# Layer two's weights as scaled float16 halves, the attention's split ahead by GpSimd and kept in DRAM

## The chip, the core and the metric

The kernel runs on one core of a Trainium2 chip. A core has five engines with an instruction queue each: TensorE (PE, matrix multiplication; its weight loads are shown apart as PEld), VectorE (DVE), ScalarE (ACT), GpSimd (POOL) and SyncE (SP), which here issues every DMA. Data lies in SBUF (128 partitions), PE writes into PSUM banks, and inputs, outputs and scratch lie in DRAM. The metric is the device time of one execution in microseconds (us). Before the change it is 1198.7 us, the median of three runs (1198.53 to 1199.05).

## What is computed

A trunk of two layers over 1024 tokens of width 1024. Each layer projects its input with `w_in` (1024 x 3072: main, memory queries, main gate, memory gate), runs a main mixer and a cross-attention of four heads into 256 memory tokens, gates both and projects them with `w_out`; then comes a residual and a layer norm.

```python
def mixer_sublayer(x, mem, w_in, w_mem_kv, w_out, main_fn):
    h = x @ w_in
    u_main = h[..., :D_MAIN]
    q_mem = h[..., D_MAIN:D_MIX]
    g_main = h[..., D_MIX:D_MIX + D_MAIN]
    g_mem = h[..., D_MIX + D_MAIN:]
    y_main = main_fn(u_main)
    y_mem = memory_attention(q_mem, mem, w_mem_kv)
    y = jnp.concatenate([y_main * jax.nn.silu(g_main), y_mem * jax.nn.silu(g_mem)], axis=-1)
    return y @ w_out
...
    x = layer_norm(ALPHA * x + y, ln_g[layer], ln_b[layer])
```

Layer one's main mixer is a causal pooling over four windows with a linear map for each group of channels. Layer two's is FoX, attention of 16 heads of 64 with a forget gate: `logit[t,s] = q_t.k_s/8 + cum[t] - cum[s]` for s up to t, where `cum` is the running sum of log-sigmoid gates. Keys, values and gates come from one projection of layer two's input, `w_kv_shared`.

## The kernel before

**Products of float32 accuracy.** A float32 matrix is split into a high and a low part, and a product is three matmuls: high x high, low x high, high x low (`three`, L217). High parts are float32r, low parts bfloat16. A split is an ACT cast for the high part and a DVE subtraction for the low one (`hi_lo`, L186); in FoX both are done by POOL (`gp_hi_lo`, L198), because `low[0]` is true there.

**Slabs.** A slab (L233) is 128 output columns of a projection, for all tokens: its weight (512 KB) is loaded by SP in two pieces of 256 KB, each split as above, and 48 matmuls of 512 columns follow, 24 for each half of the tokens (L253), into the two `pj` banks of PSUM. Layer two has 38 slabs: 24 of `w_in`, 8 for keys and 6 for values; the values of the first two pairs of heads come with the gates from a projection of 272 columns (`v_first`, L830). Layer two's input stands turned (channels in the partitions) in `XH` (float32r) and `XL` (bfloat16), made by `turned_rows` (L342) from each of eight row tiles after the layer norm: two float16 halves, two DMA transposes, and three passes by ACT, DVE and POOL (L351 to L353) into `XH` and `XL`.

**Order of the work.** Layer one's pool groups and its memory attention fill the first 327 us, `out_proj.rest` (L558) with the layer norm reaches to 454, layer two's memory queries and memory projections to 518, memory attention to 588, the first values' projection to 611, the slabs of the first keys and queries to 638; then FoX runs to about 1085, with the remaining slabs between its own matmuls, and layer two's output projection follows. PE's instructions run in the order in which the code issues them (`manual_schedule`); a planner orders the other engines' queues, and each queue runs strictly in order. In memory attention the gates' slabs 20 to 23 are filled in between the steps of the attention; a step is one tile of 128 tokens, with its softmax for four heads (L429 to L440).

**FoX's start.** For each head the running sums are read back into all partitions (tile `R`), POOL masks the diagonal block of `R` (`affine_select`, L978), and DVE adds `R` to the logits and takes the running maximum (L986). The logits lie in three PSUM banks named `L`.

Of the kernel before, what the change touches and what calls it, by code (L numbers as in the profile page):

```python
# [18 lines left out]
P = 128  # L19
S = 1024  # L20
# [22 lines left out]
class InPlace(tuple):  # L43

    pass

# [53 lines left out]
def trunk_kernel(ctx, tc, x, xT, memT, win, wk, wv0, wv, wmk, wmv, wout, poolw, pscale, lng, lnb, bforget, out):  # L100
# [107 lines left out]

    ident = const.tile([P, P], F32, name="ident")
# [23 lines left out]
    def slab(pieces_dram, XH, XL, evac, banks=("pj", 2), make=wt):  # L233

        ready = isinstance(pieces_dram, list)
        if ready:
            ws = pieces_dram
        else:
            ws = [split_w(pieces_dram[0], [P, 4, P], make=make)]
            yield 0  # L240
            ws.append(split_w(pieces_dram[1], [P, 4, P], make=make))
            yield 0

        def terms(n, kts):
            cols = slice(n * NH, (n + 1) * NH)
            out = []
            for kt in kts:
                h, l = ws[kt // 4]
                out.append(three((h[:, kt % 4, :], cut(l, slice(None), kt % 4)), (XH[:, kt, cols], cut(XL, slice(None), kt, cols))))
            return out  # L250

        def put(acc, a, b, start, stop):
            nc.tensor.matmul(acc, a, b, start=start, stop=stop)  # L253
            since[0] += NH

# [11 lines left out]
        for n in range(2):  # L267
# [5 lines left out]
            for j, (a, b) in enumerate(order):  # L273
                put(acc, a, b, j == 0, j == len(order) - 1)
                if j == len(order) - 1:
                    evac(slice(n * NH, (n + 1) * NH), acc)
                yield NH
# [3 lines left out]
    def gate(acc, dst):  # L281

        nc.scalar.activation(dst, acc, AF.Tanh, scale=0.5)
        nc.vector.scalar_tensor_tensor(dst, dst, 1.0, acc, ALU.add, ALU.mult)  # L284

    def mem_kv(l):
# [11 lines left out]
        def project(w_dram):  # L298
# [3 lines left out]
            for pc in range(2):  # L302
                a, b = split_w(w_dram[pc], [P, 4, P], nc.gpsimd if l and not pc else nc.vector)
# [13 lines left out]
        def vals(h):  # L317
            scaled_halves(
                project(wmv[l, h]), [two[:, h, 2 * e : 2 * e + 2, :].rearrange("p m t -> p (m t)") for e in range(2)],
                undo[:, h : h + 1],  # L320
# [6 lines left out]
    def scaled_halves(u, halves, un, by_tile=lambda t: t):  # L327
# [9 lines left out]
        nc.vector.tensor_scalar(un, e, 2.0 ** -15 / PSCALE, None, ALU.mult)  # L337
# [4 lines left out]
    def turned_rows(z, rows, scale, XH, XL, half, whole):  # L342

        sc, un = scale
        hi, lo = (half() for _ in range(2))
        nc.scalar.activation(hi, z, AF.Copy, scale=sc)
        nc.vector.scalar_tensor_tensor(lo, z, sc, hi, ALU.mult, ALU.subtract)
        t = whole()
        nc.sync.dma_start_transpose(t[:, :KT, :], hi)
        nc.sync.dma_start_transpose(t[:, KT:, :], lo)  # L350
        nc.scalar.activation(XH[:, :, rows], t[:, :KT, :], AF.Copy, scale=un)  # L351
        nc.vector.tensor_scalar(XL[0][:, :, rows], t[:, KT:, :], un, None, ALU.mult)
        nc.gpsimd.tensor_scalar(XL[1][:, :, rows], XH[:, :, rows].bitcast(F32), 1.0, 1.0, ALU.mult, ALU.mult)  # L353

    def norm_scale(gb):
# [10 lines left out]
        nc.vector.tensor_scalar(un[:, 1:2], e, 2.0 ** -14, None, ALU.mult)  # L366
        return un[:, 0:1], un[:, 1:2]

    def gate_units(w_dram, dst, XH, XL):
        return slab(w_dram, XH, XL, lambda cols, acc: gate(acc, (dst[0] if isinstance(dst, list) else dst)[:, cols]))  # L370

    def mem_attention(l, XH, XL, kv, qtile, ytile, yd):
# [3 lines left out]
        def query_units(h, make):  # L376
            qh, ql = qs[h]
            return slab(win[l, 8 + h], XH, XL, lambda cols, acc: hi_lo(qh[:, cols], cut(ql, slice(None), cols), acc), make=make)

        def aside_homes():  # L380

            lows = sb([P, 4, 4, P], "P", 5, BF16)
            for n in range(2):
                highs = sb([P, 2, 4, P], "P", 5, F32R)
                left = [[highs[:, k], lows[:, 2 * n + k]] for k in range(2)]
                yield lambda shape, dt=F32R, left=left: left[0].pop(0) if dt == F32R else left.pop(0)[0]

        if l:
            homes = aside_homes()
            units = [query_units(h, wt if h < 2 else next(homes)) for h in range(MH)]  # L390
            for two in units:
                run(islice(two, 2))
            while turns:
                turns.pop(0)(lambda: vt([P, D], F16), lambda: vt([P, 2 * KT, P], F16))
            for two in units:
                run(islice(two, 3 * KT))
            kv = mem_kv(l)
        (kh, kl, v, undo), keys, vals = kv
        for h in range(MH):
# [4 lines left out]
            else:  # L404
                qs.append(in_place(qtile, [P, S]))
                run(query_units(h, wt))
# [7 lines left out]
        for h in range(MH):  # L414
            fill.add(gate_units(win[l, 20 + h], gs[h], XH, XL), SLAB)
# [57 lines left out]
    class OutProj:  # L473
# [63 lines left out]
        def ordered(self, order, c):  # L537
            firsts, lasts = ({id(acc): j for j, (acc, _) in way} for way in (reversed(list(enumerate(order))), enumerate(order)))
            for j, (acc, (y, w)) in enumerate(order):
                nc.tensor.matmul(  # L540
                    acc, y, w, start=c == 2 and j == firsts[id(acc)] and acc is not self.seeded,
                    stop=c == 1 and j == lasts[id(acc)], skip_group_check=acc is self.seeded,
                )
# [14 lines left out]
        def rest(self, resid, XH, XL, dst):  # L558
# [14 lines left out]
            for sp, c in order + [(sp, c) for sp in range(2, ST // 2) for c in (2, 0, 1)]:  # L573
# [12 lines left out]
                for turn in turns if c == (1 if at_end else 0) else ():  # L586
                    turn(lambda: sb([P, D], "raw", 4, F16), lambda: T([P, 2 * KT, P], F16))
                turns = [] if c == 1 else turns
                if at_end and c == 0:
# [6 lines left out]
    def norm(sp, accs, gb, resid, scale, XH, XL, dst, seeded):  # L596
        turns = []
        for a in range(2):
# [30 lines left out]
            if XH is not None:  # L629

                def turn(half, whole, z=z, rows=rows):
                    turned_rows(z, rows, scale, XH, XL, half, whole)
# [47 lines left out]
    with tc.tile_pool(name="in0", bufs=1) as in0:  # L680
# [65 lines left out]
        for g in range(1, 4):  # L746
            pool_group(g)
            out_proj.split((4, 12, 12)[g - 1])

        XH1, XL1 = xs()  # L750
        turns = out_proj.rest(x, XH1, XL1, x1)
# [3 lines left out]
    XH, XL = XH1, XL1  # L755
    with tc.tile_pool(name="in1", bufs=1) as in1:
# [497 lines left out]
```

## Time and profile before

| | us |
|---|---|
| median of three runs | 1198.7 |
| profiled execution | 1198.79 |
| its span in the profile | 1197.0 |
| PE busy | 1172.2 |
| DVE busy | 800.5 |
| ACT busy | 616.9 |
| POOL busy | 208.4 |

The span is what the profile shows of the execution; the rest of its time lies around it. Busy time counts instructions only, not waits. In lists of instructions, the columns are: start and duration in us, engine, line of the code, operation, output and inputs by the program's names, shapes, number of instructions put together, and in brackets the idle time before them with what ended it. In groups the columns are line, engine, operation, names, shapes and number, then busy time in us and the mean of one in ns, then the idle time before them. In tables by stage a pair is busy time and number of instructions, in the order PE, PEld, DVE, ACT, POOL; behind them stand PE's granted clock (1.00 is full), the DMA engines' busy share and GB/s.

### The profile page before, as it was taken

How to read it: one execution, taken by the hardware profiler on the slowest of the kernel's cores; microseconds unless marked ns; L12 is line 12 of the kernel's file. 1: busy time of each engine (PE TensorE's matmuls, PEld its weight loads, DVE VectorE, ACT ScalarE, POOL GpSimd, SP SyncE). 2: the span in 40 equal slices, each digit the busy share in tenths (PEclk: the TensorE clock that was granted, in tenths of full speed). 3: DMA queues.
4: the chain of work that ended last, by engine and by line, in shares of the span. 5: the costliest groups of instructions: out<-in, count | busy, mean ns of one | idle time of the engine just before them, and what ended most of it. 6: DMA issues, size and time to landing. Idle time of an engine off the chain costs nothing. (4 is left out here: it accounts for less than half of the span.)

```text
span 1197.0 us, 19472 instructions
## 1 busy us (share of the span) xinstructions
PE 1172.2 (98%) x6810; PEld 739.3 (62%) x6927; DVE 800.5 (67%) x1864; ACT 616.9 (52%) x1330; POOL 208.4 (17%) x312
## 2 busy tenths in 40 slices
PE   9999999999999999999999999999999999999997
PEld 4567665555555555677776666666666666655554
DVE  6544767374656576377546888778878888874654
ACT  7433654262532224366325777767766787773110
POOL 2000000000000000200103334333334324530000
PEclk9999999999999999999999999999999999999999
DMA  7333654242355666355526789879897999976431
GB/s 246 115 101 87 131 115 159 79 123 80 102 197 158 159 156 161 106 138 100 171 54 161 152 199 173 195 155 195 187 186 164 195 191 210 230 206 229 154 116 48
DMA packets 280803, 182.06 MB, mean 152 GB/s; under 512 B 225024, under 2 KB 238976, under 8 KB 280704
## 3 DMA queue, kind: packets, MB, share of 16 engines
q1 hardware_dynamic: 280704, 180.81, 62.0%
q8 instruction: 54, 0.88, 0.3%
q14 instruction: 45, 0.37, 0.1%
HBM read 95.24 MB, written 22.61 MB: 98 GB/s over the span
## 5 line engine op out<-in xcount | busy, mean ns | idle before, releaser
L253 PE MATMUL pj<-A,w 128*128 128x512 bf16 (+1 forms) x1817 | 571.4, 398 | 2.2 <-DVE B L894 1.1
L253 PE MATMUL pj<-A,wl 128*128 128x512 bf16 x929 | 351.8, 380 | 6.4 <-issue 3.4
L253 PEld LDWEIGHTS pj<-A,w 128*128 128x128 f32 x944 | 174.8, 188 | 45.4 <-POOL wl L200 2.0
L253 PEld LDWEIGHTS <-w 128*128 128x128 bf16 x960 | 93.1, 98 | 121.3 <-issue 39.4
L253 PEld LDWEIGHTS <-wl 128*128 128x128 bf16 x960 | 94.3, 98 | 87.9 <-issue 4.2
L994 ACT ACTIVATE T<-MK,s 128x512 f32<-128x512 f32 x192 | 111.0, 578 | 44.5 <-DVE s L986 22.6
L1015 ACT ACTIVATE P<-T,s 128x512 f16<-128x512 f32 x192 | 103.1, 576 | 52.8 <-issue 26.3
L1016 DVE SCALAR_TENSOR_TENSOR P<-T,s,P 128x512 f16<-128x512 f32 x192 | 112.3, 612 | 24.0 <-ACT P L1015 22.3
L540 PEld LDWEIGHTS <-T 128*128 128x128 bf16 x736 | 70.6, 98 | 88.9 <-issue 6.8
L190 DVE TENSOR_TENSOR wl<-raw,w 128x512 bf16<-128x512 f32 (+1 forms) x96 | 67.9, 713 | 72.3 <-ACT w L189 69.7
L231 PE MATMUL L<-B,B 128*128 128x512 f32 (+3 forms) x384 | 109.0, 386 | 4.6 <-DVE s L986 4.2
L189 ACT CAST w<-raw 128x512 fp32r<-128x512 f32 (+1 forms) x104 | 62.8, 609 | 84.0 <-PE pj L253 57.6
L231 PEld LDWEIGHTS L<-B,B 128*128 128x128 f32 x384 | 71.1, 189 | 29.6 <-DVE s L986 9.9
L353 POOL TENSOR_SCALAR A<-A 128x1024 bf16<-128x1024 f32 x8 | 8.4, 1049 | 444.5 <-ACT A L351 427.9
L986 DVE CUSTOM_DVE_ANT_0 MK<-L,R 128x512 f32<-128x512 f32 (+3 forms) x128 | 72.8, 569 | 8.4 <-PE L L231 5.6
L978 POOL TENSOR_SCALAR_AFFINE_SELECT R<-R 128x128 f32<-128x128 f32 x128 | 42.2, 335 | 207.4 <-DVE s L986 162.5
L200 POOL TENSOR_TENSOR wl<-raw,w 128x512 bf16<-128x512 f32 x54 | 69.4, 1285 | 3.8
L190 DVE TENSOR_TENSOR T<-T,T 128x1024 bf16<-128x1024 f32 x23 | 31.6, 1374 | 48.1 <-ACT T L189 48.0
L189 ACT CAST T<-T 128x1024 fp32r<-128x1024 f32 x23 | 24.1, 1047 | 71.7 <-DMA T<-y1d 45.4
L199 POOL TENSOR_SCALAR w<-raw 128x512 fp32r<-128x512 f32 x54 | 35.9, 665 | 58.5 <-PE pj L253 58.5
L540 PE MATMUL L<-B,T 128*128 128x512 bf16 (+1 forms) x163 | 43.1, 391 | 0.3
L433 ACT ACTIVATE P<-L,s 128x256 f32<-128x256 f32 x64 | 29.6, 474 | 23.4 <-issue 13.0
(296 smaller groups left out, 1789.7 us busy)
## 6 DMA issues: line engine op xcount, KB each, us to landing
raw<-in_win_dram SPq DMA_DIRECT2D x94, 256.0 KB, 2.9
raw<-in_wout_dram SPq DMA_DIRECT2D x40, 256.0 KB, 2.9
B<-B SPq DMA_DIRECT2D x32, 256.0 KB, 4.5
R<-cumd SPq DMA_DIRECT2D x16, 512.0 KB, 4.6
T<-y0d SPq DMA_DIRECT2D x12, 512.0 KB, 5.1
y0d<-Y SPq DMA_DIRECT2D x11, 512.0 KB, 2.7
T<-y1d SPq DMA_DIRECT2D x11, 512.0 KB, 4.7
raw<-in_wmk_dram SPq DMA_DIRECT2D x16, 256.0 KB, 2.7
```

Source lines behind the costliest of these rows:

```text
L189: pin(nc.scalar.copy(hi, src))
L190: pin(by.tensor_tensor(lo[0], src, hi.bitcast(F32), ALU.subtract))
L199: nc.gpsimd.tensor_scalar(hi, src, 1.0, 1.0, ALU.mult, ALU.mult)
L200: nc.gpsimd.tensor_tensor(lo[0], src, hi.bitcast(F32), ALU.subtract)
L231: nc.tensor.matmul(acc, a, b, start=i == 0, stop=i == len(terms) - 1)
L253: nc.tensor.matmul(acc, a, b, start=start, stop=stop)
L540: nc.tensor.matmul(acc, y, w, start=c == 2 and j == firsts[id(acc)] and acc is not self.seeded, stop=c == 1 and j == lasts[id(acc)], skip_ ...
L978: nc.gpsimd.affine_select(R[:, qs], R[:, qs], [[-1, P]], ALU.is_ge, -NEG, base=0, channel_multiplier=1).ins
L986: nc.vector.tensor_tensor_reduce(p[:, lo:up], lg, R[:, lo:up], 1.0, top, ALU.add, ALU.min, m[:, n : n + 1])
L994: nc.scalar.activation(e, p[:, lo:up], AF.Exp, bias=top, scale=-1.0, accum_out=sums[:, n, hd % 2, i : i + 1],)
L1015: nc.scalar.activation(pair[:, lo:up], e, AF.Copy, scale=r)
L1016: nc.vector.scalar_tensor_tensor(pair[:, L + lo : L + up], e, r, pair[:, lo:up], ALU.mult, ALU.subtract)
```

## The change

**Float16 halves in layer two.** `turned_rows` transposes the two float16 halves straight into one tile `X1`, so that the three passes behind the transposes are gone. All of layer two's slabs and `v_first` take float16 halves of the weights too, scaled by one power of two for all weights. The three matmuls stay three, now all float16, with the tokens' side read as four strips of 128. The scale is undone where each product is evacuated.

**The scale.** `look_over` loads all 38 slabs and the four pieces of the first values' projection once more, in layer one, and DVE takes each one's largest magnitude: 16 loads lie beside pool groups one and two, 26 beside the output projection. `weight_scale` brings the maxima of the partitions together through DRAM.

**Split ahead.** `prepared` takes 27 slabs in the order in which FoX needs them. For each, POOL issues the load, multiplies by the scale, rounds to float16, subtracts, and issues the store of both halves to DRAM. FoX then loads halves in place of raw weights, and POOL's splits there are gone. The other 11 slabs are split by ACT and DVE as they are used. Two smaller things move from POOL to DVE: eight subtractions in the memory projections, and the building of the constant tiles `later` and `ones`.

```diff
+    def split_f16(src, make):
+        t = make()
+        hi, lo = t[:, 0], t[:, 1]
+        nc.scalar.activation(hi, src, AF.Copy, scale=wscale[0])
+        nc.vector.scalar_tensor_tensor(lo, src, wscale[0], hi, ALU.mult, ALU.subtract)
+        return hi, (lo, hi)
...
+    def prepared(spare):
+        waiting, lows = [], []
+        def stored():
+            key, out = waiting.pop(0)
+            nc.gpsimd.dma_start(ready[key][0].ap.rearrange("c p e k m -> p c e (k m)"), out)
+        for n, key in enumerate(in_order()):
...
+            with tc.issue_after(lows[n - 3]) if n > 2 else nullcontext():
+                nc.gpsimd.dma_start(r, src.rearrange("c p k m -> p c (k m)"))
+            sc = wscale[0].unsqueeze(2).to_broadcast([P, 2, NH])
+            nc.gpsimd.tensor_tensor(r, r, sc, ALU.mult)
+            nc.gpsimd.tensor_scalar(out[:, :, 0], r, 1.0, 1.0, ALU.mult, ALU.mult)
+            lows.append(nc.gpsimd.tensor_tensor(out[:, :, 1], r, out[:, :, 0], ALU.subtract).ins)
+            waiting.append((key, out))
+            if len(waiting) > 2:
+                with tc.issue_after(lows[-1]):
+                    stored()
+            yield
...
-    def turned_rows(z, rows, scale, XH, XL, half, whole):
-        sc, un = scale
-        hi, lo = (half() for _ in range(2))
-        nc.scalar.activation(hi, z, AF.Copy, scale=sc)
-        nc.vector.scalar_tensor_tensor(lo, z, sc, hi, ALU.mult, ALU.subtract)
-        t = whole()
-        nc.sync.dma_start_transpose(t[:, :KT, :], hi)
-        nc.sync.dma_start_transpose(t[:, KT:, :], lo)
-        nc.scalar.activation(XH[:, :, rows], t[:, :KT, :], AF.Copy, scale=un)
-        nc.vector.tensor_scalar(XL[0][:, :, rows], t[:, KT:, :], un, None, ALU.mult)
-        nc.gpsimd.tensor_scalar(XL[1][:, :, rows], XH[:, :, rows].bitcast(F32), 1.0, 1.0, ALU.mult, ALU.mult)
+    def turned_rows(z, tile_of, sc, X, half):
+        for e in range(2):
+            t = half()
+            if e == 0:
+                hi = t
+                nc.scalar.activation(hi, z, AF.Copy, scale=sc)
+            else:
+                nc.vector.scalar_tensor_tensor(t, z, sc, hi, ALU.mult, ALU.subtract)
+            nc.sync.dma_start_transpose(X.t[:, e, tile_of], t)
...
+    def look_over():
...
+        def reduced():
+            n, t = landed.pop(0)
+            nc.vector.tensor_reduce(tops[:, n : n + 1], t, AX.X, ALU.max, apply_absolute_value=True)
...
-                a, b = split_w(w_dram[pc], [P, 4, P], nc.gpsimd if l and not pc else nc.vector)
+                a, b = split_w(w_dram[pc], [P, 4, P], nc.vector)
...
-        nc.gpsimd.memset(ones, 1.0)
-        nc.gpsimd.memset(later, 0.0)
-        for k in range(1, ST):
-            nc.gpsimd.affine_select(later, later, [[1, P]], ALU.not_equal, 1.0, base=-k * HEADS, channel_multiplier=-1)
+        nc.vector.memset(ones, 1.0)
+        nc.vector.memset(later, 0.0)
+        for k in range(HEADS, P, HEADS):
+            nc.vector.tensor_tensor(later[:, k:], later[:, k:], ident[:, : P - k], ALU.add)
...
             run(start_units(*own, keys))
+            run(prep[0])
+            prep[0] = None
             low[0] = True
             fox(following, out_proj)
```

POOL's queue before, from the end of layer one to FoX's first mask (`L978 AFFINE_SELECT R`). `L353` is the last pass of a turned row, `L190` a subtraction of the memory projections, `L774` to `L777` build the constant tiles, `L199` and `L200` split the first weight pieces for FoX:

```order
L353 TENSOR_SCALAR A_3076<-A_3075 128x8x128 x8
L190 TENSOR_TENSOR wl_4334<-raw_4331,w_4333 128x512
L190 TENSOR_TENSOR wl_4374<-raw_4371,w_4373 128x512
...
L774 MEMSET G_5564 128x128
L775 MEMSET G_5564 128x128
L777 AFFINE_SELECT G_5564<-G_5564 128x128 x7
L199 TENSOR_SCALAR w_6164<-raw_6162 128x512
L200 TENSOR_TENSOR wl_6165<-raw_6162,w_6164 128x512
L199 TENSOR_SCALAR w_6170<-raw_6168 128x512
L200 TENSOR_TENSOR wl_6171<-raw_6168,w_6170 128x512
L978 AFFINE_SELECT R_6139<-R_6139 128x128
```

The same stretch of POOL's queue after the change; the mask is now at L1157. `L271` is a load's issue, `L273` the multiplication by the scale (`unrow`), `L274` the rounding, `L275` the subtraction, `L263` a store's issue; the rows left out are the items between the first and the last:

```order
L271 DMA A_3154<-in_win_dram 128x2x512 x3
L273 TENSOR_TENSOR A_3154<-A_3154,unrow 128x1024 x2
L274 TENSOR_SCALAR A_3154<-A_3154 128x2x512 x2
L275 TENSOR_TENSOR A_3154<-A_3154 128x2x512 x2
...
L263 DMA half_104<-A_3154 128x2x1024
L274 TENSOR_SCALAR A_3154<-A_3154 128x2x512
L263 DMA half_106<-A_3154 128x2x1024
L275 TENSOR_TENSOR A_3154<-A_3154 128x2x512
L263 DMA half_105<-A_3154 128x2x1024
L263 DMA half_107<-A_3154 128x2x1024
L1157 AFFINE_SELECT R_6348<-R_6348 128x128 x8
```

All 27 items and their 54 DMA issues have come between the layer norm and the first mask.

DVE's queue before, in the output projection, at the row tiles four and five (`L347` is a turned row's subtraction, `L627` the layer norm's last step, `L352` the second pass of a turned row):

```order
L618 TENSOR_SCALAR s_3820<-s_3819,s_3817 128x1
L347 SCALAR_TENSOR_TENSOR raw_3899<-G_3787,unrow,raw_3898 128x1024
L619 TENSOR_SCALAR s_3820<-s_3820 128x1
L620 TENSOR_TENSOR s_3819<-s_3819,s_3820 128x1
L627 SCALAR_TENSOR_TENSOR G_3809<-G_3809,s_3819,P_3155 128x1024
L347 SCALAR_TENSOR_TENSOR raw_3909<-G_3809,unrow,raw_3908 128x1024
L352 TENSOR_SCALAR A_3076<-T_3902,unrow 128x8x128
L352 TENSOR_SCALAR A_3076<-T_3912,unrow 128x8x128
```

The same place of DVE's queue after; the turned row's subtraction is now L447, the layer norm's last step L787, and L510 to L514 and L468 work the scale out:

```order
L510 TENSOR_REDUCE s_3961<-raw_3960 128x1
L779 TENSOR_SCALAR s_3940<-s_3940 128x1
L447 SCALAR_TENSOR_TENSOR raw_4034<-G_3907,unrow,raw_4031 128x1024
L780 TENSOR_TENSOR s_3939<-s_3939,s_3940 128x1
L511 TENSOR_SCALAR s_3961<-s_3961 128x1
L787 SCALAR_TENSOR_TENSOR G_3929<-G_3929,s_3939,P_3233 128x1024
L512 TENSOR_SCALAR s_3962<-s_3961 128x1
L513 RECIPROCAL unrow<-s_3962 128x1
L468 TENSOR_TENSOR unrow<-unrow,s_3962 128x1
L514 TENSOR_SCALAR unrow<-unrow 128x1
...
L447 SCALAR_TENSOR_TENSOR raw_4040<-G_3929,unrow,raw_4037 128x1024
```

The scale, for which POOL's first multiplication waits, is ready between the subtractions of row tiles four and five.

More of the change, by code (lines that the diff above doesn't have):

```diff
@@ L45, with __init__, at @@
     pass
+class Ready:
+    def __init__(self, ap):
+        self.ap = ap
+class Tiled:
+    def __init__(self, t):
+        self.t = t
+    def at(self, kt, cols):
+        a, b = cols.start // P, cols.stop // P
+        hi, lo = (self.t[:, e, a, kt, :] if b == a + 1 else self.t[:, e, a:b, kt, :] for e in range(2))
+        return hi, (lo, hi)
 class Fill:
@@ L539, in ordered @@
             for j, (acc, (y, w)) in enumerate(order):
-                nc.tensor.matmul(
+                ins = nc.tensor.matmul(
                     acc, y, w, start=c == 2 and j == firsts[id(acc)] and acc is not self.seeded,
                     stop=c == 1 and j == lasts[id(acc)], skip_group_check=acc is self.seeded,
-                )
+                ).ins
+                if look[0] and j % 16 == 8:
+                    with tc.issue_after(ins):
+                        next(look[0], None)
                 yield NH
@@ L629, in norm, with turn @@
             if XH is not None:
-                def turn(half, whole, z=z, rows=rows):
-                    turned_rows(z, rows, scale, XH, XL, half, whole)
+                def turn(half, z=z, s=s):
+                    turned_rows(z, s, scale, XH, half)
                 turns.append(turn)
```

197 lines of the change are left out of this document (152 added, 45 removed).

## The prediction

> **What bounds the kernel now.** I read the page's head and busy times first, then busy time by stage, then single instructions on PE, POOL and DVE.
>
> ```profile
> span 1197.0 us, 19472 instructions
> ...
> PE 1172.2 (98%) x6810; PEld 739.3 (62%) x6927; DVE 800.5 (67%) x1864; ACT 616.9 (52%) x1330; POOL 208.4 (17%) x312
> ```
>
> ```profile
> core 0: us, PE busy (x) PEld busy (x) DVE busy (x) ACT busy (x) POOL busy (x), PEclk, DMA share, GB/s
> ...
> 326.00:417.00 91.00, 90.56 (x404) 52.91 (x411) 54.34 (x84) 29.11 (x37) 4.19 (x4) 1.00 0.62 179
> 433.00:636.00 203.00, 201.85 (x1273) 137.69 (x1291) 117.22 (x267) 91.26 (x223) 23.59 (x25) 1.00 0.52 130
> ```
>
> ```profile
> 518.00:588.00 70.00, 69.44 (x500) 47.09 (x507) 52.71 (x135) 44.64 (x131) 5.39 (x9) 1.00 0.59 132
> ```
>
> PE is busy 98% at full clock, so every microsecond its instructions lose or gain is the kernel's. Up to FoX, POOL is nearly empty: 23.6 of the 203 us between the end of layer one and FoX. DVE is not: in memory attention (518 to 588) it works 52.7 of 70 us, 17.3 free. The sum is made against the profiled execution, 1198.79 us (span 1197.0 plus 1.8 around it); the runs' median, 1198.7, is the same to 0.1.
>
> **The gain: PE.** All 38 slabs of layer two get 48 float16 matmuls in place of 16 float32r and 32 bfloat16 ones.
>
> ```profile
> 187.36 3.34 PE L253 MATMUL pj<-A,w 128*128 128x512 f32 x13
> ...
> 197.98 3.34 PE L253 MATMUL pj<-A,w 128*128 128x512 f32 x13
> ...
> 208.60 1.74 PE L253 MATMUL pj<-A,w 128*128 128x512 f32 x6
> ```
>
> ```profile
> 705.10 0.38 PE L253 MATMUL pj<-A,w 128*128 128x512 bf16 x1
> 705.32 0.38 PE L253 MATMUL pj<-A,wl 128*128 128x512 bf16 x1
> ```
>
> These PE rows are read by their starts (first column): from one slab's first float32r matmul to the next slab's, 48 matmuls, 10.62 us pass. Neighbouring bfloat16 matmuls start 0.216 apart, so 48 need 10.37: 0.25 saved a slab. Float16 and the tiled input in four strips of 128 have no row at 512 columns; bounds are the bfloat16 pitch and the float32r one ((10.62 - 32 x 0.216) / 16 = 0.23). I take bfloat16's, nearest in bytes. 38 x 0.25 = 9.6; the first values' projection has 64 float32r matmuls of 272 columns: 64 x 272/512 x 0.016 = 0.5. Together **-10.2** (bounds -10.2 and 0). About 3.4 of it falls ahead of FoX, 6.8 in it.
>
> **The look over the weights.** 42 more loads (some 21 MB) and 42 DVE reductions in layer one; 26 of them in 326 to 417.
>
> ```profile
> L332 DVE TENSOR_REDUCE s<-MK 128x1 f32<-128x1024 f32 x6 | 7.3, 1216 | 0.0
> ```
>
> 26 x 1.22 = 32 us bring DVE from 54 to 86 of 91 us. 26 x 0.52 MB in 91 us is 150 GB/s on 179; at the stage's 0.62 share for 179 the DMA share becomes about 1.1, 10 us too much at worst. Against it stand transfers loaded several tiles ahead, and shorter work per turned row (no second ACT, DVE and POOL pass). I take **+2**, bounds 0 and 10. The other 16 lie in pool groups with time to spare and cost nothing; if that cover went, DVE would be late with the pooled tiles.
>
> **Two moves to DVE.** The memory projections' 8 subtractions leave POOL, the two constant tiles' eight builders too. They are small beside DVE's free time and are counted below with what blocks DVE.
>
> **POOL's preparation.** 27 slabs, each a load, a multiplication, a rounding, a subtraction and a store, wait for the weight scale, which DVE computes between the subtractions of turned rows four and five (of zero to seven); the row below is the fifth. All 27 stand on POOL ahead of FoX's first mask, so whoever waits for the mask waits for all of them: the DVE logits (L986), then PE.
>
> ```profile
> 433.09 1.28 DVE L347 SCALAR_TENSOR_TENSOR raw<-G,unrow,raw 128x1024 f16<-128x1024 f32 x1 [1.22 <-ACT raw L346]
> ```
>
> ```profile
> L200 POOL TENSOR_TENSOR wl<-raw,w 128x512 bf16<-128x512 f32 x54 | 69.4, 1285 | 3.8
> L199 POOL TENSOR_SCALAR w<-raw 128x512 fp32r<-128x512 f32 x54 | 35.9, 665 | 58.5 <-PE pj L253 58.5
> ...
> L1083 POOL TENSOR_TENSOR R<-R,G 128x256 f32<-128x256 f32 x12 | 8.5, 733 | 9.0 <-DVE G L284 3.6 <-DMA R<-y1d 3.2 <-DVE s L1007 2.2
> L353 POOL TENSOR_SCALAR A<-A 128x1024 bf16<-128x1024 f32 x8 | 8.4, 1049 | 444.5 <-ACT A L351 427.9 <-ACT s L616 16.6
> ```
>
> ```profile
> 344.44 0.53 SPq L582 DMA_DIRECT2D T<-y0d  x1
> ...
> 363.64 1.28 SPq L349 DMA_TRANSPOSE T<-raw  x1
> ```
>
> ```profile
> T<-y0d SPq DMA_DIRECT2D x12, 512.0 KB, 5.1
> ```
>
> From 733 ns at 256 columns and 1285 at 512, a two-tensor instruction of 1024 takes 1285 + 512 x 2.16 = 2.39 us (bounds 1.05, if the scale read as a broadcast costs like L353, and twice 1285 = 2.57). An item is 2.39 + 1.05 + 2.39 = 5.83, 27 are 157 us (bounds 121 and 167). The trace has no DMA issued by POOL: bounds are SP's 0.53 for 512 KB and 1.28, its dearest issue. I take 1.0, nearer the upper one, because software on POOL writes what SP's hardware does; 54 of them are 54 us (29 and 69). Five times a round begins with its loads and waits for one to land, 5.1 less other issues, about 3: 12 to 15 us. Sum about 223 us: from 433 POOL is free at 656.
>
> **The shared port.** That sum assumes that POOL and DVE don't touch each other. These rows say that they do.
>
> ```profile
> 489.28 1.28 POOL L190 TENSOR_TENSOR wl<-raw,w 128x512 bf16<-128x512 f32 x1 [2.95 <-ACT w L189]
> ```
>
> ```profile
> 490.02 1.08 DVE L190 TENSOR_TENSOR wl<-raw,w 128x512 bf16<-128x512 f32 x1
> ```
>
> ```profile
> 533.61 0.68 DVE L190 TENSOR_TENSOR wl<-raw,w 128x512 bf16<-128x512 f32 x1
> ```
>
> ```profile
> 792.29 1.60 POOL L199 TENSOR_SCALAR w<-raw 128x512 fp32r<-128x512 f32 x1
> ```
>
> ```profile
> 791.37 2.03 DVE L340 SCALAR_TENSOR_TENSOR MK<-MK,s,MK 128x1024 f16<-128x1024 f32 x1 [0.60 <-ACT MK L339]
> ```
>
> DVE's subtraction of two SBUF tensors takes 0.68 alone, but 1.08 when POOL is in a subtraction that ends at 490.56: it moved only then. At 791.37 a DVE instruction with two SBUF inputs took 2.03 behind a POOL one, and POOL's next, 0.67 on average, took 1.60 behind DVE. Each waits for the other's whole instruction. So POOL's 2.4 us instructions, one after another from 433 on, stand in DVE's way.
>
> ```profile
> L440 DVE SCALAR_TENSOR_TENSOR P<-P,s,P 128x256 f16<-128x256 f32 x32 | 13.5, 480 | 1.2 <-ACT P L439 1.2
> ...
> L190 DVE TENSOR_TENSOR wl<-raw,w 128x512 bf16<-128x512 f32 x8 | 5.5, 687 | 0.3
> ...
> L470 DVE TENSOR_TENSOR V<-V,G 128x1024 f32<-128x1024 f32 x3 | 3.7, 1233 | 0.1
> L190 DVE TENSOR_TENSOR MK<-raw,MK 128x272 bf16<-128x272 f32 x8 | 3.2, 443 | 0.0
> ```
>
> ```profile
> 531.36 1.66 DVE L440 SCALAR_TENSOR_TENSOR P<-P,s,P 128x256 f16<-128x256 f32 x4
> ```
>
> These groups of 518 to 588 read two SBUF tensors: some 52 instructions (with L470's fourth). POOL's cycle is 5.83 + 2 x 1.0 + 0.5 = 8.3 us; a lone arrival waits (2.39 x 2.39 x 2 + 1.05 x 1.05) / (2 x 8.3) = 0.75 on average. L440 comes in fours: the first waits 0.75, each next up to one POOL instruction (mean 1.94), about 1.5 since DMA issues leave gaps. 8 x (0.75 + 4.5) = 42, 20 lone ones 15: 57 us, against 17 free. Behind them stand softmax (L429, L436), the evacuations (L284) and so PE's banks: about 40 late. Ahead of 518 some 40 such instructions cost 30 us in a stage with more free time: 0 to 15, I take none. Bounds of this term: 22, if every wait is a lone one (52 x 0.75 - 17), and 57.
>
> POOL itself loses some of each of the 100 or so DVE instructions of some 0.5 us between 433 and 636: I take half, 0.25, since the other half falls into its DMA issues and waits. 656 + 25 = 681. Against this stands when FoX needs its first mask, in POOL's, DVE's and PE's rows:
>
> ```profile
> 636.15 0.29 POOL L978 TENSOR_SCALAR_AFFINE_SELECT R<-R 128x128 f32<-128x128 f32 x1 [6.73 <-DMA R<-cumd]
> ```
>
> ```profile
> 638.71 0.69 DVE L986 CUSTOM_DVE_ANT_0 MK<-L,R 128x512 f32<-128x512 f32 x1 [3.11 <-PE L L231]
> ```
>
> ```profile
> 637.87 1.27 PE L231 MATMUL L<-B,B 128*128 128x512 f32 x4
> ...
> 641.46 1.16 PE L231 MATMUL L<-B,B 128*128 128x512 f32 x4
> ...
> 643.00 0.38 PE L818 MATMUL L<-s,G 1*128 1x1 f32 x2
> ...
> 643.79 1.05 PE L231 MATMUL L<-B,B 128*128 128x512 f32 x4
> ```
>
> Three L banks are filled at 637.87, 641.46 and 643.00; the fourth user, at 643.8 (640.4 after the early gain of 3.4), needs the first one back. That comes 1.3 us after POOL is free (mask 0.29, DVE 0.69, their hand-overs): 681 + 1.3 - 640.4 = 42 late. The two delays are not added: time lost in memory attention is time given to POOL. The later one counts, **+40**.
>
> By the Trainium skill (SBUF — State Buffer, Who interferes with whom), two SBUF inputs are what makes a DVE instruction clash with GpSimd, while one with at most one SBUF input outside the two-port modes doesn't. L440 alone has no row beside POOL here; without it the stage would lose 15 us, less than is free, and only POOL's lateness would remain.
>
> **FoX.** 54 splits (69.4 + 35.9 us) leave POOL there; the halves come in as many SP loads of 256 KB, and with a slab or more ahead they stay hidden; if not, PE waits some 3 us at a slab. Less blocking of DVE: **-2**, bounds 0 and -4.
>
> Sum: -10.2 + 2 + 40 - 2 = +29.8, so 1198.8 + 29.8, about **1229**.
>
> **Rivals.**
> - *POOL is late, but DVE isn't held up* (the waits fall into DVE's and PE's slack). POOL free at 656, 17 us late: 1198.8 - 10.2 + 2 - 2 + 17 = 1205. For it: PE runs some steps ahead of the softmax. Against: the 2.03 row. Chance 0.13.
> - *The preparation fits* (other side, faster). POOL done within 206 us of 433 and DVE's mean wait under 17.3/52 = 0.33 us: 1188.6. It decides if a POOL DMA costs 0.53 and the multiplication 1.05 (121 + 29 + 12 = 162 us, free at 595, plus blocking). Chance 0.14; another 0.04 for landing within 0.2% of before, about what a measurement of this kernel can tell from no change.
> - *PE cools down.* In the row below nine matmuls from standstill take 4.0 us, where nine at 0.216 take 1.9. Eight attention steps that each stand still some 5 us would pay up to 2 each, halved since not all reach that: +8, 1237; with the upper bounds of POOL's prices up to 1255. Chance 0.14.
> - *Float16 brings nothing* (the strips cost what float32r did): 1239. Chance 0.05.
>
> ```profile
> L120 PE MATMUL idle<-warm 128*128 128x512 bf16 x9 | 4.0, 631 | 1.2 <-DVE warm L117 1.2
> ```
>
> The Trainium skill (TensorE: Matmul & The Clock Gate) has the clock fall to half only after a whole idle window, about 3.4 us; by that, stalls in shorter pieces cost no clock at all, and 1229 stands.
>
> **Numbers.** The forecast has 0.50 (own range 1214 to 1246). Faster: 0.14 plus 0.03 for a rival-one case with a short lateness, 0.17. Same 0.04. Slower 0.79. The range, 1194 to 1255, leaves out the fitting case and stalls beyond every bound.
>
> **What would show it.** Slab starts 10.4 apart; POOL full from about 433 to 680 with 2.4 us multiplications; L440's fours over 4 us in place of 1.66; PE idle in 518 to 640, named after DVE; the first mask near 680. I am wrong if POOL ends before 635, or if L440 stays near 0.48 beside a busy POOL; then the time falls to 1189 to 1206.

## The result, and the profile after

The changed kernel takes 1300.5 us (median of four runs, 1298.2 to 1305.8) against 1198.6 (four runs): a ratio of 1.0856, 95% interval 1.0821 to 1.089. It is slower, as forecast, but by 102 us and not by 30, and the time lies far outside the range of 1194 to 1255.

The page of the changed kernel, its head and its busy times:

```profile
span 1299.7 us, 19621 instructions
...
PE 1193.6 (92%) x6927; PEld 697.2 (54%) x6927; DVE 926.6 (71%) x1925; ACT 612.2 (47%) x1318; POOL 264.2 (20%) x314
```

Busy time by stage, while POOL prepares the slabs (453 to 668), in the table's columns as before:

```profile
core 0: us, PE busy (x) PEld busy (x) DVE busy (x) ACT busy (x) POOL busy (x), PEclk, DMA share, GB/s
453.00:518.00 65.00, 43.00 (x169) 19.21 (x168) 44.69 (x52) 15.26 (x24) 56.45 (x38) 0.82 0.82 215
518.00:668.00 150.00, 102.07 (x622) 63.40 (x620) 119.84 (x140) 49.09 (x124) 124.51 (x94) 0.85 0.71 199
```

PE is busy 145 of these 215 us, so it stands still for 70, while DVE too is idle for 50 of the 215; PE's granted clock is 0.82 to 0.85, where it was 1.00 before. What PE waited for longest (engine, tile and line, then the releaser, total us, number, longest):

```profile
PE L L315 <- ACT P L586: 34.7, 5, 9.6
PE pj L340 <- DVE B L532: 19.6, 2, 14.8
PE L L693 <- DVE G L771: 12.2, 1, 12.2
PE L L315 <- DVE s L1165: 9.4, 14, 1.5
PE T L315 <- DMA T<-P: 8.1, 1, 8.1
```

L586 is the softmax's exponential; it waits for DVE's maximum of its step. L771 is the layer norm of layer one, on the third pair of row tiles. The groups of DVE's instructions from 453 to 668 tell why DVE is late:

```profile
L593 DVE SCALAR_TENSOR_TENSOR P<-P,s,P 128x256 f16<-128x256 f32 x24 | 38.4, 1649 | 1.6 <-ACT P L592 1.5
L209 DVE TENSOR_TENSOR wl<-raw,w 128x512 bf16<-128x512 f32 x16 | 30.5, 1917 | 9.1 <-ACT w L208 9.0
...
L583 DVE TENSOR_SCALAR s<-s 128x2 f32<-128x2 f32 x14 | 12.2, 885 | 0.0
...
L589 DVE TENSOR_SCALAR s<-s 128x4 f32<-128x4 f32 x6 | 6.2, 1036 | 5.1 <-ACT P L586 4.9
L532 DVE SCALAR_TENSOR_TENSOR B<-pj,unrow,B 128x512 bf16<-128x512 f32 x8 | 5.9, 746 | 9.8 <-ACT B L531 9.7
```

L593 is L440 of before: 1649 ns in place of 480. L209, the weight's subtraction, takes 1917 in place of some 690. Even the scalings of 2 or 4 columns (L583, L589) take 885 and 1036, where before (518 to 588) they took 162 and 170:

```profile
L430 DVE TENSOR_SCALAR s<-s 128x2 f32<-128x2 f32 x16 | 2.4, 162 | 0.0
...
L436 DVE TENSOR_SCALAR s<-s 128x4 f32<-128x4 f32 x8 | 1.4, 170 | 8.1 <-ACT P L433 8.1
```

L532, which reads one input from PSUM, takes 746 and is not lengthened: 749 in the run below that has the look over the weights and prepares nothing. One lengthened instruction in DVE's list, and POOL's list at the same time:

```profile
598.89 10.83 DVE L593 SCALAR_TENSOR_TENSOR P<-P,s,P 128x256 f16<-128x256 f32 x1 [0.64 <-ACT P L592]
609.64 0.68 DVE L582 TENSOR_REDUCE s<-L 128x2 f32<-128x512 f32 x1
```

```profile
598.69 3.75 POOL L273 TENSOR_TENSOR A<-A,unrow 128x1024 f32<-128x1024 f32 x2
602.41 2.05 POOL L274 TENSOR_SCALAR A<-A 128x1024 f16<-128x1024 f32 x2
604.43 2.11 POOL L275 TENSOR_TENSOR A<-A 128x1024 f16<-128x1024 f32 x1
606.49 0.78 POOL L263 DMA_DIRECT2D half<-A  x1
607.29 2.13 POOL L275 TENSOR_TENSOR A<-A 128x1024 f16<-128x1024 f32 x1
609.36 0.74 POOL L263 DMA_DIRECT2D half<-A  x1
```

DVE's 0.48 us of work began 0.2 us behind the start of a POOL instruction and ended at 609.72: it waited through six POOL instructions, the first of them already running, and one DMA issue, and got through in POOL's next issue. POOL itself went through its 27 items nearly as estimated (its groups from 453 to 668), and the first mask was not late because of it:

```profile
L275 POOL TENSOR_TENSOR A<-A 128x1024 f16<-128x1024 f32 x27 | 59.8, 2215 | 0.4
L273 POOL TENSOR_TENSOR A<-A,unrow 128x1024 f32<-128x1024 f32 x27 | 53.8, 2001 | 67.2 <-DVE unrow L514 43.1 <-DMA A<-in_win_dram 14.1 <-DMA A<-in_wk_dram 7.3
L274 POOL TENSOR_SCALAR A<-A 128x1024 f16<-128x1024 f32 x27 | 32.1, 1197 | 0.3
L263 POOL DMA_DIRECT2D half<-A x27 | 20.4, 755 | 0.0
```

```profile
741.06 0.29 POOL L1157 TENSOR_SCALAR_AFFINE_SELECT R<-R 128x128 f32<-128x128 f32 x1 [74.21 <-DMA R<-cumd]
```

POOL was free 74 us before the running sums had come for its first mask. FoX starts 105 us late (741.06 against 636.15) because PE came late. Lastly the clock, in PE's list behind two of the stalls:

```profile
500.97 7.18 PE L340 MATMUL pj<-A,P 128*128 128x512 f16 x24 [14.77 <-DVE B L532]
512.96 8.00 PE L340 MATMUL pj<-A,P 128*128 128x512 f16 x24 [4.80 <-DVE B L532]
521.50 10.52 PE L340 MATMUL pj<-A,w 128*128 128x512 f16 x48 [0.54 <-issue]
```

24 float16 matmuls take 7.2 and 8.0 us behind a stall; 48 of them take 10.5 with PE warm, which makes 5.3 for 24. The Trainium skill (TensorE: Matmul & The Clock Gate) has the clock come back only after some microseconds of work; the trace agrees, with 2 to 3 us lost at each of these stalls.

### The profile page after: what moved, and what is told of

Its sections match the earlier page's. It is cut to its first block, busy times and chain, and to the rows that moved or that the text cites. A ratio compares the mean times of both kernels' runs of the same rounds, so it can differ in the third digit from the quotient of the medians.

```text
span 1299.7 us, 19621 instructions
## 1 busy us (share of the span) xinstructions
PE 1193.6 (92%) x6927; PEld 697.2 (54%) x6927; DVE 926.6 (71%) x1925; ACT 612.2 (47%) x1318; POOL 264.2 (20%) x314
## 5 line engine op out<-in xcount | busy, mean ns | idle before, releaser
L340 PE MATMUL pj<-A,w 128*128 128x512 f16 (+2 forms) x2464 | 642.9, 389 | 4.3 <-DVE w L232 2.4
L340 PEld LDWEIGHTS <-w 128*128 128x128 f16 (+1 forms) x2112 | 193.0, 99 | 240.5 <-issue 40.9
L340 PE MATMUL pj<-A,wl 128*128 128x512 bf16 x368 | 138.5, 379 | 0.3 <-ACT A L215 0.3
L1157 POOL TENSOR_SCALAR_AFFINE_SELECT R<-R 128x128 f32<-128x128 f32 x128 | 41.9, 333 | 388.2 <-DVE s L1165 257.6
L209 DVE TENSOR_TENSOR wl<-raw,w 128x512 bf16<-128x512 f32 (+1 forms) x86 | 78.1, 918 | 59.1 <-ACT w L208 57.5
L271 POOL DMA_DIRECT2D A<-in_win_dram x15 | 11.3, 753 | 389.9 <-DVE s L780 386.5
L208 ACT CAST w<-raw 128x512 fp32r<-128x512 f32 (+1 forms) x86 | 51.8, 608 | 72.0 <-PE pj L340 53.8
L340 PEld LDWEIGHTS pj<-A,w 128*128 128x128 f32 x368 | 68.6, 189 | 18.9 <-issue 0.7
L209 DVE TENSOR_TENSOR T<-T,T 128x1024 bf16<-128x1024 f32 x23 | 31.4, 1366 | 66.2 <-ACT T L208 66.2
L273 POOL TENSOR_TENSOR A<-A,unrow 128x1024 f32<-128x1024 f32 x27 | 53.8, 2001 | 67.2 <-DVE unrow L514 43.1
L315 PE MATMUL L<-MK,B 128*128 128x256 bf16 (+1 forms) x192 | 31.1, 327 | 34.7 <-ACT P L586 34.7
L586 ACT ACTIVATE P<-L,s 128x256 f32<-128x256 f32 x64 | 29.6, 472 | 67.1 <-DVE s L583 31.8
L275 POOL TENSOR_TENSOR A<-A 128x1024 f16<-128x1024 f32 x27 | 59.8, 2215 | 0.4
L593 DVE SCALAR_TENSOR_TENSOR P<-P,s,P 128x256 f16<-128x256 f32 x64 | 55.6, 918 | 4.7 <-ACT P L592 4.6
```

The costliest lines, as they stand in the source:

```text
L208: pin(nc.scalar.copy(hi, src))
L209: pin(by.tensor_tensor(lo[0], src, hi.bitcast(F32), ALU.subtract))
L273: nc.gpsimd.tensor_tensor(r, r, sc, ALU.mult)
L275: lows.append(nc.gpsimd.tensor_tensor(out[:, :, 1], r, out[:, :, 0], ALU.subtract).ins)
L315: nc.tensor.matmul(acc, a, b, start=i == 0, stop=i == len(terms) - 1)
L340: ins = nc.tensor.matmul(acc.rearrange("p (s t) -> p s t", t=P) if tiled else acc, a, b, start=start, stop=stop).ins
```

## The experiments

Theory A: POOL's long instructions shut DVE out of the SBUF port, DVE is late in layer two's start, and PE with it. Theory B: POOL's DMAs, 28 MB more, hold SP's loads up. Open besides were the cost of the look over the weights, the gain of the float16 matmuls, and how long DVE is shut out. Float16 alone was run seven times, with the look twice, with the look but without its trip through DRAM eight times; every other experiment stands on one run, and the changed kernel's four runs spread over 7.6 us, so smaller differences between single runs say little.

**Float16 alone.** Nothing is prepared ahead and nothing looked over; weights have no scale.

```diff
-        nc.scalar.activation(hi, src, AF.Copy, scale=wscale[0])
-        nc.vector.scalar_tensor_tensor(lo, src, wscale[0], hi, ALU.mult, ALU.subtract)
+        if low[0]:
+            nc.gpsimd.tensor_scalar(hi, src, 1.0, 1.0, ALU.mult, ALU.mult)
+            nc.gpsimd.tensor_tensor(lo, src, hi, ALU.subtract)
+        else:
+            nc.scalar.copy(hi, src)
+            nc.vector.tensor_tensor(lo, src, hi, ALU.subtract)
...
-    ready = {key: two_of(dram.tile([2, P, 2, 4, P], F16, name=nm("half"))) for key in in_order()}
+    ready = {}
...
```

> Layer two's float16 halves alone: weights without a scale (high part rounded to float16, low part the rest), no look over the weights, nothing prepared ahead; POOL splits in FoX as in the kernel before, ACT and DVE elsewhere. Theory A: the float16 matmuls are worth what the slab pitch says, 38 x 0.25 = 9.6 us, and nothing else changes: 1198.6 - 9.6 = 1189 (1186 to 1193). Rival C (the gain does not come, because FoX is held by DVE and the float16 slabs only wait there; the changed kernel's lateness shrank by 3 us from memory attention to the end): 1193 to 1199.

Measured: 1194.8 us, ratio 0.9967 (0.9955 to 0.9978). It beats the kernel before, by 4 us and not by 9.6. (The two moves from POOL to DVE are in this run too.) The first logits reach DVE at 634.7, 4.0 earlier than before; from there to the last logits 418.7 us pass against 419.2. The page's busy times of this run, and one line each of PE's waits in the kernel before and in this run:

```profile
span 1192.3 us, 19427 instructions
...
PE 1168.0 (98%) x6873; PEld 689.1 (58%) x6927; DVE 800.1 (67%) x1878; ACT 609.9 (51%) x1314; POOL 178.3 (15%) x287
```

```profile
PE L L231 <- DVE s L986: 4.2, 9, 1.0
```

```profile
PE L L319 <- DVE s L1170: 10.3, 15, 1.5
```

Ahead of FoX the gain is there in full. In FoX PE's slabs are shorter, and PE waits 6.1 us longer for DVE's logits: this is rival C of the expectation.

**POOL's DMAs alone.**

```diff
-            nc.gpsimd.tensor_tensor(r, r, sc, ALU.mult)
-            nc.gpsimd.tensor_scalar(out[:, :, 0], r, 1.0, 1.0, ALU.mult, ALU.mult)
-            lows.append(nc.gpsimd.tensor_tensor(out[:, :, 1], r, out[:, :, 0], ALU.subtract).ins)
+            nc.gpsimd.tensor_tensor(r[:, :, :2], r[:, :, :2], sc[:, :, :2], ALU.mult)
+            nc.gpsimd.tensor_scalar(out[:, :, 0, :2], r[:, :, :2], 1.0, 1.0, ALU.mult, ALU.mult)
+            lows.append(nc.gpsimd.tensor_tensor(out[:, :, 1, :2], r[:, :, :2], out[:, :, 0, :2], ALU.subtract).ins)
...
```

> The changed kernel with POOL's three instructions per slab cut from 1024 columns to 4 (two of each piece), and with the stores taken from layer two's input; all 54 of POOL's DMAs, their bytes and their order stay, so FoX gets wrong weights. Theory A (POOL's long instructions hold the SBUF port that DVE needs): PE loses only the 16 to 18 us in layer one's output projection and keeps the float16 gain of up to 10, so about 1200 to 1215. Theory B (28 MB more on the DMA engines, or POOL's DMA issues, delay the loads): little changes, 1270 to 1300.

Measured: 1254.4, between the two theories. Its lists of SP and of ACT show what is left:

```profile
457.26 15.81 SPq L244 DMA_DIRECT2D raw<-in_win_dram  x6
```

```profile
469.57 0.72 ACT L231 ACTIVATE w<-raw,unrow 128x512 f16<-128x512 f32 x1 [17.88 <-DMA raw<-in_win_dram]
```

Without the long instructions POOL issues its DMAs faster: 50 of them between 453 and 580 us, where the changed kernel issues 51 between 467 and 666. The first loads of the query slabs take 11.9 to 12.6 us to land, against 2.5 to 4.8 in the changed kernel, and ACT stands idle for 17.9 us until they have. That stall may belong to the bunched DMAs, so the run was made again at a slower pace.

**POOL's DMAs alone, paced.** As before, but the short multiplication reads a column that ACT copies from each half slab's result.

```diff
+    def step(acc):
+        at = 42 + len(paced) % 22
+        nc.scalar.activation(tops[:, at : at + 1], acc[:, :1], AF.Copy, scale=0.0)
+        paced.append(at)
...
-            nc.gpsimd.tensor_tensor(r[:, :, :2], r[:, :, :2], sc[:, :, :2], ALU.mult)
+            at = paced[-1]
+            nc.gpsimd.tensor_tensor(
+                r[:, :, :2], r[:, :, :2], tops[:, at : at + 1].unsqueeze(2).to_broadcast([P, 2, 2]), ALU.mult,
+            )
```

> As the run with POOL's DMAs alone (its three instructions per slab cut to 4 columns, stores from layer two's input, FoX's weights wrong), but each of POOL's items now waits for an evacuated half slab of PE (ACT copies one column, times zero, into a tile that POOL's short multiplication reads), so that the 54 DMAs are spread over layer two's start as in the changed kernel and not bunched into its first 100 us. Theory A (the port; the 60 us left in the bunched run came of the bunching): 1194.8 for float16 alone + 18.6 for the look = 1213 (1208 to 1225). Theory B (28 MB more by POOL's queue hold SP's loads up at any pace): 1240 to 1260.

Measured: 1227.0, 2 us above theory A's range and 13 below theory B's. The same loads land in 2.8 to 4.1 us. Of PE's waits in this run, one is the copy's own:

```profile
PE L L708 <- DVE G L786: 11.2, 1, 11.2
PE pj L353 <- ACT tops L302: 5.9, 2, 3.4
```

Less these 5.9, 1221. With the look at 1211.5 (below), POOL's DMAs at this pace cost 10 to 16 us; the whole preparation costs 89 (1300.5 - 1211.5).

**POOL's instructions alone.** Of POOL's 54 DMAs one store stays; the multiplication writes into the output tile, so that it doesn't scale a tile twice.

```diff
-            with tc.issue_after(lows[n - 3]) if n > 2 else nullcontext():
-                nc.gpsimd.dma_start(r, src.rearrange("c p k m -> p c (k m)"))
...
-            nc.gpsimd.tensor_tensor(r, r, sc, ALU.mult)
+            nc.gpsimd.tensor_tensor(out.bitcast(F32).rearrange("p c e m -> p c (e m)"), r, sc, ALU.mult)
...
-            waiting.append((key, out))
-            if len(waiting) > 2:
+            if n == 0:
+                waiting.append((key, out))
...
```

> The changed kernel with one load-store pair of POOL's DMAs in place of 27: all 81 instructions of POOL stay at full length and run on what lies in the tiles, and FoX loads the one stored slab every time, so its weights are wrong. Theory A (the port): still 1270 to 1310, possibly with a shorter but denser disturbance, since without DMA issues and waits POOL's instructions follow each other without a gap for 27 x 5.4 = 146 us. Theory B (DMAs): falls to 1200 to 1220.

Measured: 1332.2, more than the changed kernel itself and above theory A's range. DVE's list and PE's wait:

```profile
458.21 122.60 DVE L232 SCALAR_TENSOR_TENSOR w<-raw,unrow,w 128x512 f16<-128x512 f32 x2 [7.27 <-ACT w L231]
580.73 0.68 DVE L770 SCALAR_TENSOR_TENSOR G<-G,pj 128x512 f32<-128x512 f32 x1
```

```profile
PE pj L339 <- DVE G L770: 115.0, 1, 115.0
```

POOL's groups of this run: 27 instructions each of 2.11, 1.92 and 1.05 us, with at most 0.1 us between them. Two DVE instructions of 0.75 us stand there for 122.6; the second (459.36 to 580.81) is passed over by 73 of POOL's and gets in when two of POOL's run of 81 are left. With next to no DMAs of POOL's the time rises: theory B alone is out, and so is the theory that DVE always gets the port at the next boundary.

**Shorter instructions.**

```diff
-            nc.gpsimd.tensor_tensor(r, r, sc, ALU.mult)
+            for q in range(4):
+                c, m = q // 2, slice(256 * (q % 2), 256 * (q % 2) + 256)
+                nc.gpsimd.tensor_tensor(r[:, c, m], r[:, c, m], sc[:, c, m], ALU.mult)
...
```

(The rounding and the subtraction likewise.)

> The changed kernel with each of POOL's three instructions per slab cut into four of 256 columns: the same work and bytes in 324 instructions. If DVE gets the port at the next instruction boundary (the prediction's theory), its waits shrink to a third (POOL's instructions last 0.73 and some 0.35 us in place of 2.2 and 1.05): the 87 us that POOL costs fall to some 40, 1250 (1235 to 1265). If a waiting DVE instruction is passed over for as long as POOL's instructions follow each other without a pause, only POOL's total time counts, and that grows by the shorter instructions' overhead: 1290 to 1350.

Measured: 1281.5, between the two ranges. POOL's multiplications and subtractions last 0.71 and 0.75 us, its roundings 0.48. Summing over the stretch from POOL's first multiplication to the first mask what each DVE instruction took above the shortest of its kind and shape in that stretch gives 58 us here and 84 in the changed kernel. In the changed kernel 41 of the 48 waits of more than 0.2 us touch one or two of POOL's instructions and issues, the others three to seven; here 47 of 60 do, the others three to eight, one 17. So DVE sometimes gets the next boundary and sometimes is passed over; what decides it stays open.

The same sum follows the cost of the preparation from run to run. Against the fitting run without preparation (1211.5 with the look, 1194.8 without), 125 us of added DVE time go with 121 us of cost in POOL's instructions alone, 84 with 89 in the changed kernel, 58 with 70 here, 43 with 38 in the next run, and 5 with 16 in the paced run of POOL's DMAs; float16 with the look, without any preparation, has 3. The bunched run is the exception, 4 with 43: there loads were late, and DVE's instructions kept their length.

**Fewer instructions.** No look, no scale; POOL rounds and subtracts only.

```diff
-            nc.gpsimd.tensor_tensor(r, r, sc, ALU.mult)
+            if n < 3:
+                nc.gpsimd.tensor_tensor(r[:, :, :2], r[:, :, :2], sc[:, :, :2], ALU.mult)
...
```

> The changed kernel without the look over the weights and without a scale: POOL's multiplication by the scale is gone (a copy of 2 x 2 columns of it stays for the first three slabs, so that POOL starts at the same place), its rounding, subtraction and all DMAs stay: 27 x 3.2 = 87 us of long instructions in place of 146. Theory A: POOL's cost, 87 us, falls in proportion or faster, since the pauses for landing loads grow: 1194.8 + 30 to 52 = 1225 to 1247. If the DMAs are what costs, it stays at the 1282 of the run without the look.

Measured: 1232.4, as theory A had it: 37.6 above float16 alone, where the run with the multiplication (the first of the next ones) stands 87.1 above it. The 27 multiplications, 54 us on POOL, carry some 50 us of the kernel. Here no wait touches more than three POOL instructions. The DVE group that was at 1649, in this run from 518 to 640:

```profile
L590 DVE SCALAR_TENSOR_TENSOR P<-P,s,P 128x256 f16<-128x256 f32 x32 | 16.9, 583 | 1.9 <-ACT P L589 1.8
```

**The look.** First, without it in the changed kernel:

```diff
-                look[0] = look_over()
+                look[0] = iter(())
...
-        nc.sync.dma_start(row, topd[0].partition_broadcast(P))
-        nc.vector.tensor_reduce(m, row, AX.X, ALU.max)
+        nc.vector.tensor_scalar(m, landed_tile, 0.0, 0.5, ALU.mult, ALU.add)
```

> The changed kernel without the look over the weights: no 42 loads, no 42 reductions, no trip of the maxima through DRAM; the scale is the constant that the inputs give, worked out by DVE at the same place from a tile that lands there. Theory A: the 17.7 us that the matmuls are late at the end of layer one's output projection go, the disturbance by POOL stays, so 1300.5 - 17 = 1283 (1275 to 1290). Rival: the look and the preparation hurt by the same DMA load, and without the look the memory attention recovers too: under 1260.

Measured: 1281.9, as theory A had it: without the look 18.6 us go, and the preparation still costs 87.1 above float16 alone, so the look's DMA load is not what makes it dear. Then with the look, without the trip of the maxima through DRAM:

```diff
-        m = tiny(1)
-        nc.vector.tensor_reduce(m, tops[:, : len(parts)], AX.X, ALU.max)
-        nc.sync.dma_start(topd.rearrange("a p -> p a"), m)
```

> The changed kernel with the look's 42 loads and 42 reductions, but without the trip of the maxima through DRAM: the scale is a constant made at the same place. If the 12.2 us stall at the end of layer one's output projection comes of the trip (its read back stands ahead of a tile's load on SP's queue and waits for the write), most of the 18.6 us go: 1286 to 1292. If it comes of the look's loads (26 of them fill the DMA engines to 1.01 of their time between 330 and 362), it stays at 1298 to 1303.

Measured: 1299.5, within the spread of the changed kernel, which looks as if the trip cost nothing. But PE's wait for the layer norm did fall, from 12.2 to 3.8 us; the waits in the preparation grew. The two can't be told apart beside the preparation, so both were run on float16 alone. There the look was put back in full:

```diff
+                look[0] = look_over()
...
-        nc.vector.tensor_scalar(sc, sc, 2.0 ** 14, None, ALU.mult)
+        nc.vector.tensor_scalar(sc, sc, 0.0, 1.0, ALU.mult, ALU.add)
+        nc.vector.tensor_scalar(e, e, 0.0, 2.0 ** 14, ALU.mult, ALU.add)
```

> The float16 kernel that prepares nothing ahead (1194.8), with the look over the weights put back: 42 loads, 42 reductions, the maxima's trip through DRAM and the scale's small DVE steps (the scale itself is set to one after that). If the look costs by itself what its removal from the changed kernel gave, 1194.8 + 18.6 = 1213; if only what PE waited for in its stretch of the changed kernel (12.2 for the layer norm and 2.6 for a pool group's bank), 1209.6. Under 1203 would say that most of the 18.6 was the preparation's, by other timing.

Measured: 1211.5 (two runs), so the look costs 16.7 us. And without the trip, taken out by the edit shown above for the changed kernel:

> The same without the trip through DRAM (the maxima stay unused, the scale is made of a constant at the same place). If the trip's two transfers on SP's queue hold back the tile's load that PE waits for, the 12.2 us fall to the 3.8 us seen in the changed kernel without the trip: 1201 (1199 to 1203). If the 26 loads do it, within 2 us of the run with the trip.

Measured: 1201.9 (eight runs, 1199.0 to 1205.4): the trip costs 9.6 us, the 42 loads and reductions 7.1. SP's list of the changed kernel, and PE's at the place, show how the trip does it:

```profile
411.15 9.29 SPq L448 DMA_TRANSPOSE A<-raw  x2
420.50 0.58 SPq L504 DMA_DIRECT2D topd<-s  x1
421.17 0.38 SPq L762 DMA_DIRECT2D G<-in_x_dram  x1
421.64 0.55 SPq L738 DMA_DIRECT2D T<-y0d  x1
430.03 0.33 SPq L509 DMA_DIRECT2D raw<-topd  x1
430.46 0.53 SPq L738 DMA_DIRECT2D T<-y0d  x1
```

```profile
439.62 3.78 PE L693 MATMUL L<-B,T 128*128 128x512 f32 x8 [12.16 <-DVE G L771]
```

The read back (L509) stands ahead of a tile's load (L738) on SP's queue and waits 7.8 us for the write (L504) to land; the load goes out at 430.46, DVE's split of that tile (L209) can't run before 437.70, and the layer norm that PE needs (L771) stands behind the split on DVE.

## Why the prediction was wrong

**The direction and the mechanism were right, the size was not.** The sum was -10.2 + 2 + 40 - 2. Measured, by the runs: float16 -4.0, the look +16.7, the preparation +89 (1300.5 - 1211.5), of which POOL's DMAs at the paced rate 10 to 16 and POOL's instructions the rest by subtraction, 73 to 79. The parts don't add up freely: without DMAs between them POOL's instructions cost 121. Most of the signs that the prediction named came as well: POOL was full until 667 and L440's fours took four times 1.65 us; only the first mask came at 741 and not near 680.

**The step that failed: "57 us, against 17 free ... about 40 late", and ahead of 518 "0 to 15, I take none".** DVE's added time was sized nearly right: 57 + 30 = 87 us in the working, 84 in the trace. What was wrong is that DVE's free time would absorb half of it: 17 of the 57 in memory attention, and ahead of 518 all of the 30. It absorbed next to nothing: nearly all of the 84 us came out at PE, and from 453 to 668 DVE was still idle for 50 us while PE stood still for 70. The likely reason, read from the waits and not tested apart, is that DVE's idle time lies in waits for ACT and PE, which wait for DVE in turn: a late instruction moves the whole chain, and the idle time comes again behind it. That the 87 came so near the 84 is partly luck. I had left out the scalings (L583 and L589, 15 us above their time), and "each waits for the other's whole instruction" was no upper bound: most waits touch one or two POOL instructions, one touched six and an issue, and in the run without DMAs one was passed over by 73.

**"POOL is late for the mask".** POOL's prices were near: multiplication 2.00 for 2.39, rounding 1.20 for 1.05, subtraction 2.22 for 2.39, a DMA's issue 0.75 for 1.0; 213 us from 453.6 to 666.8 for 223. But the mask waited for the running sums, not for POOL, so this second delay, from which the +40 was taken as the later one, never came to count.

**"The look: +2, bounds 0 and 10".** It was 16.7, beyond the bound. I priced its loads and reductions (7.1, within the bounds) and not the trip of the maxima, two small transfers on an in-order queue that hold a tile's load up (9.6).

**"PE cools down", a rival at +8.** It came true and larger: of the 107 us between the spans of the changed kernel and of float16 alone (1299.7 - 1192.3), some 82 are waiting and some 26 (1193.6 - 1168.0) slower matmuls. It is no cause of its own: the clock is low where PE stalls, and the stalls are the preparation's and the look's.

**"The gain: -10.2".** The pitch was right (0.216 between float16 matmuls, four strips and all), and the 3.4 ahead of FoX came as 4.0. The 6.8 in FoX came as 0.5: there PE took to waiting for DVE's logits what its slabs saved. I had read PE's 98% as if "every microsecond its instructions lose or gain is the kernel's".

**"FoX: -2".** From the first logits to the last 417.5 us passed in the changed kernel, against 418.7 in float16 alone: -1.2, within the bounds.

**The range.** It reached to 1255 with a cooled PE and the upper bounds of POOL's prices, while the port's term was let go no higher than 57, which is memory attention's part alone. With 87 in place of 40 and the look's 16.7 in place of 2 the sum gives 1290, still 10 short of the time; the gain that failed to come in FoX is most of what is left.

## What to carry to other kernels

An engine that looks idle in the busy table is not free if it shares an SBUF port with the engine that paces the stage: count the pacing engine's instructions that read two SBUF tensors, and its scalings from SBUF to SBUF, and take the other's back-to-back run as the wait that one of them may meet. Idle time of an in-order engine inside a chain of waits isn't slack; take it off a delay only where a row shows work that runs ahead. A small round trip through DRAM on a queue costs what is queued behind its wait, and a gain on PE counts only in stages where no other engine's results set the pace.

## What the runs showed of the hardware

- A DVE instruction that waits for the port isn't always served when POOL's current instruction ends. It waited through six POOL instructions and a DMA issue (10.83 us for 0.48 us of work), and was passed over by 73 POOL instructions that ran without pauses (121 us for 0.75 us of work). Cutting POOL's instructions into quarters took DVE's added time from 84 to 58 us, not to a quarter.
- Not only two-tensor instructions wait: scalings of 2 columns took 0.89 us on average in place of 0.16. By the Trainium skill (SBUF — State Buffer, Who interferes with whom), scalings can use both ports too, while an instruction with one SBUF input outside those modes doesn't clash; the rows agree, with L532, which reads one input from SBUF and one from PSUM, unlengthened at 746 ns.
- POOL's 54 DMA issues of 512 KB took 0.72 to 0.93 us (median 0.74) in the changed kernel and as much in the run without POOL's long instructions. In the paced run DVE's instructions took 5 us in all above their shortest beside such issues, against 3 in float16 with the look, where POOL issues none.
- With 50 of POOL's DMAs within 128 us, loads of 256 KB that SP issued took up to 12.6 us to land; with 51 within 199 us the same loads took 2.5 to 4.8.
